# Exchanging the two hardware DMA queues of a softmax mixture: loads from ScalarE, stores from SyncE

## Chip, cores, metric

One core of a Trainium2 chip. The metric is device time in microseconds (us), lower is better. The time of the kernel before was 780.9 us (median of 3, 780.88 to 781.12).

## The reference

```python
# logits (32, 128, 4, 4096) f32, prior (32, 128, 4) f32 -> out (32, 128, 4096) f32
prior_probs = softmax(prior, axis=-1)
mixture = np.sum(prior_probs[..., None] * softmax(logits, axis=-1), axis=2)
```

Each of 4096 rows has four heads of 4096 logits. 268.4 MB come in, 67.1 MB go out.

## The kernel before

The rows are cut into 32 tiles (`U`) of 128 rows. A tile is loaded as 128 rows of 64 KB, four exponentials on ScalarE give the heads and their sums, VectorE weighs and adds them into an output tile, and a store sends that out. Logits and output tiles have two buffers each. SyncE and ScalarE each have a queue (also called a ring) of transfers of their own; a transfer lands when its completion is signalled, and a packet in the profile's counts is here one contiguous row, or piece of a row, of a transfer (plus 16 tiny ones each). Waits are put in by hand: `only(ins, *keep)` lets an instruction wait for `keep` and nothing else.

```python
    def load(u):
        if u == 0 or u >= U - 3:                     # first and last tiles come in pieces
            cuts = (0, 2, 3, 4) if u == U - 1 else (0, 2, 4)
        else:
            cuts = (0, H)
        for h, to in zip(cuts, cuts[1:]):
            ld = nc.sync.dma_start(out=ltile[:, u % 2, h:to], in_=lg[u // J, u % J, :, h:to, :])
            if u >= 2:
                only(ld, adds[u - 2, 0] if h == 0 else exps[u - 2, to - 1])
            ...
    def store(u, acc, eng, lo=0, hi=V):
        st = eng.dma_start(out=ov[u // J, u % J, :, lo:hi], in_=acc[:, lo:hi])
        stores[u] = only(st, adds[u, H - 1])
    ...
        for u in range(U):
            ...
            free = (stores[u - 2],) if bufd and u >= 2 else ()
            m = H if u < U - 4 else 2                # the last four tiles work in pairs of heads
            for h in range(H):
                late = h == H - 1 and 4 <= u < U - 3
                if h == H - 1 and 0 < u < U - 3:
                    store(u - 1, obuf[:, (u - 1) % 2], nc.scalar)
                exp(h, *((stores[u - 4],) if late else ()))
                ...
                mul = weigh(g, m, *(free if g == 0 else ()))   # GpSimd; waits for the output tile
                ...                                            # then the adds, on VectorE
            if u + 2 < U:
                load(u + 2)
            if u == U - 3:                           # tiles 28, 29: stores on SyncE,
                store(u - 1, obuf[:, (u - 1) % 2], nc.sync)    # behind the last loads
                store(u, acc, nc.sync)
            elif u == U - 2:
                store(u, acc, nc.sync)
```

The softmax here doesn't subtract the row's maximum and nothing guards it: scores larger than these inputs give would overflow.

## Time and profile before

| | before |
|---|---|
| median time; span of the profiled run | 780.9; 779.3 us |
| bytes, mean rate over the span | 335.66 MB, 431 GB/s |

The prediction below shows the lines of the profile, and reads from them what bounds the kernel.

### The profile page before, as it was taken

What the parts mean: (1) busy time and instruction counts of PE and PEld (TensorE: products, weight loads), DVE (VectorE), ACT (ScalarE), POOL (GpSimd) and SP (SyncE); (2) the same over time, 40 slices, a digit from 0 to 9 for tenths busy, and PEclk for the clock granted to TensorE, in tenths of its full rate; (3) what the DMA queues carried; (4) which work ended last, traced back from release to release, by engine and by line L of the source; (5) the groups of instructions that cost most, each with busy time, mean ns of one, the idle gap of its engine ahead of it and who ended that gap; (6) DMA issues with size and microseconds to landing.
All of it is one profiled execution on the core that took longest, in us unless ns stands there. A gap on an engine that the chain in (4) does not pass through costs nothing.

```text
span 779.3 us, 654 instructions
## 1 busy us (share of the span) xinstructions
DVE 521.0 (67%) x174; ACT 466.7 (60%) x258; POOL 8.3 (1%) x41
## 2 busy tenths in 40 slices
DVE  4447875558755587555775557855578655689886
ACT  4476555775457755577555675546765567657782
POOL 0000000000000000000000000000000000000000
DMA  9999999999999999999999999999999999999998
GB/s 407 457 417 401 470 407 434 428 461 428 405 467 403 458 420 433 442 443 418 431 454 407 454 408 467 420 415 447 432 442 417 463 399 463 410 427 433 434 429 377
DMA packets 10117, 335.66 MB, mean 431 GB/s; under 512 B 1136, under 2 KB 1136, under 8 KB 1152
## 3 DMA queue, kind: packets, MB, share of 16 engines
q1 hardware_dynamic: 6048, 276.83, 82.3%
q10 hardware_dynamic: 4064, 58.79, 17.6%
q14 instruction: 5, 0.04, 0.0%
HBM read 268.50 MB, written 67.11 MB: 431 GB/s over the span
## 4 chain that ended last, share of the span: by engine, by line
DMA 64%; ACT 27%; DVE 6%; issue 2%; POOL 0%; DVEq 0%; POOLq 0%
DMA ltile<-in_logits_dram 62%; ACT ebuf L159 19%; ACT ltile L159 8%; DVE obuf L177 5%; DMA out_dram<-obuf 2%; DVE ltile L183 1%; POOL coeff L170 0%; DVE rden L168 0%; DVEq L240 0%; POOLq L240 0%; POOLq L170 0%
## 5 line engine op out<-in xcount | busy, mean ns | idle before, releaser
L183 DVE SCALAR_TENSOR_TENSOR obuf<-ebuf,coeff,obuf 128x4096 f32<-128x4096 f32 x90 | 403.6, 4484 | 3.8 <-POOL coeff L170 0.6
L159 ACT ACTIVATE ebuf<-ltile 128x4096 f32<-128x4096 f32 x90 | 322.9, 3589 | 7.4 <-DMA ltile<-in_logits_dram 7.4
L159 ACT ACTIVATE ltile<-ltile 128x4096 f32<-128x4096 f32 x38 | 137.3, 3614 | 280.6 <-DMA ltile<-in_logits_dram 280.6
L168 DVE RECIPROCAL rden<-dsum 128x4 f32<-128x4 f32 (+1 forms) x36 | 6.3, 175 | 227.9 <-ACT ebuf L159 225.1
L177 DVE TENSOR_SCALAR obuf<-ltile,coeff 128x4096 f32<-128x4096 f32 x30 | 70.6, 2353 | 10.2 <-POOL coeff L170 10.2
L183 DVE SCALAR_TENSOR_TENSOR ltile<-ltile,coeff 128x4096 f32<-128x4096 f32 (+1 forms) x7 | 27.0, 3875 | 0.8 <-POOL coeff L170 0.6
L159 ACT ACTIVATION_READ_ACCUMULATOR ebuf<-ltile 128x1 f32 x90 | 16.8, 186 | 0.0
L170 POOL TENSOR_TENSOR coeff<-rden,pp 128x4 f32<-128x4 f32 (+1 forms) x36 | 7.2, 200 | 755.3 <-DVE rden L168 745.4
L159 ACT ACTIVATION_READ_ACCUMULATOR ltile<-ltile 128x1 f32 x38 | 7.1, 186 | 0.0
L139 DVE TENSOR_REDUCE pmax<-pr 16x256 f32<-16x1024 f32 x1 | 1.2, 1208 | 7.8 <-DMA pr<-in_prior_dram 7.8
L141 ACT ACTIVATE pr<-pr 16x1024 f32<-16x1024 f32 x1 | 1.1, 1055 | 7.8 <-DVE pr L140 7.8
L177 DVE TENSOR_SCALAR ltile<-ltile,coeff 128x4096 f32<-128x4096 f32 x2 | 4.7, 2354 | 0.6 <-POOL coeff L170 0.6
L144 DVE TENSOR_TENSOR pn<-pr,pmax 16x1024 f32<-16x1024 f32 x1 | 1.9, 1939 | 0.1
L141 ACT ACT_TABLE_LOAD x1 | 1.3, 1283 | 1.2 <-PEq L229 1.2
L142 DVE TENSOR_REDUCE pmax<-pr 16x256 f32<-16x1024 f32 x1 | 1.2, 1207 | 1.1 <-ACT pr L141 1.1
L149 DVE STREAM_TRANSPOSE pp<-pn 32x256 f32<-32x256 f32 x4 | 1.7, 435 | 0.1
L143 DVE RECIPROCAL pmax<-pmax 16x256 f32<-16x256 f32 x1 | 1.7, 1741 | 0.0
L140 DVE TENSOR_TENSOR pr<-pr,pmax 16x1024 f32<-16x1024 f32 x1 | 1.2, 1211 | 0.0
L138 POOL MEMSET pn<- 32x1024 f32 x1 | 0.9, 941 | 0.3 <-POOLq L229 0.3
L229 POOL MEMSET const-bfloat16-1.0<- 128x1 bf16 x1 | 0.1, 106 | 0.0
L229 POOL MEMSET const-uint8-127<- 128x1 uint8 x1 | 0.1, 106 | 0.0
L229 POOL MEMSET const-float32-0.0<- 128x1 f32 x1 | 0.1, 103 | 0.2 <-issue 0.2
(1 smaller groups left out, 0.1 us busy)
## 6 DMA issues: line engine op xcount, KB each, us to landing
out_dram<-obuf ACTq DMA_DIRECT2D x28, 2048.0 KB, 29.4
ltile<-in_logits_dram SPq DMA_DIRECT2D x7, 4096.0 KB, 26.1
ltile<-in_logits_dram SPq DMA_DIRECT2D x2, 2048.0 KB, 30.9
out_dram<-obuf SPq DMA_DIRECT2D x2, 2048.0 KB, 33.9
out_dram<-ltile SPq DMA_DIRECT2D x1, 2048.0 KB, 17.2
out_dram<-ltile SPq DMA_DIRECT2D x2, 1024.0 KB, 4.8
ltile<-in_logits_dram SPq DMA_DIRECT2D x28, 30.9
pr<-in_prior_dram ACTq DMA_DIRECT2D x1, 64.0 KB, 7.0
```

Source lines behind the costliest of these rows:

```text
L139: nc.vector.reduce_max(pmax, pr, axis=AX.X)
L140: nc.vector.tensor_sub(pr, pr, pmax.unsqueeze(2).to_broadcast([G, R, H]))
L141: nc.scalar.activation(pr, pr, AF.Exp)
L142: nc.vector.reduce_sum(pmax, pr, axis=AX.X)
L143: nc.vector.reciprocal(pmax, pmax)
L144: nc.vector.tensor_mul(pn[0:G].rearrange("g h r -> g r h"), pr, pmax.unsqueeze(2).to_broadcast([G, R, H]))
L149: nc.vector.transpose(pp[32 * t : 32 * (t + 1)], pq[:, :, :, 32 * t : 32 * (t + 1)])
L159: ex = nc.scalar.activation(es[h], lt[:, h], AF.Exp, accum_out=dsum[:, u, h : h + 1])
L168: rc = nc.vector.reciprocal(rden[:, u, h : h + n], dsum[:, u, h : h + n])
L170: mul = nc.gpsimd.tensor_mul(coeff[:, u, h : h + n], rden[:, u, h : h + n], ppu[:, h : h + n])
L177: st = nc.vector.tensor_scalar(out=acc[:, lo:hi], in0=es[h][:, lo:hi], scalar1=coeff[:, u, h : h + 1], scalar2=None, op0=ALU.mult,)
L183: st = nc.vector.scalar_tensor_tensor(out=acc[:, lo:hi], in0=es[h][:, lo:hi], scalar=coeff[:, u, h : h + 1], in1=acc[:, lo:hi], op0=ALU.mu ...
```

## The change

The intent is to let ScalarE issue the loads and SyncE the stores and the prior, to send the first transfer of both queues ahead of the start barrier, and to wait for the output tile in the fourth exponential and not in GpSimd's coefficient.

```diff
-            ld = nc.sync.dma_start(
+            ld = nc.scalar.dma_start(
...
-        nc.scalar.dma_start(out=pr, in_=pv)
+        nc.sync.dma_start(out=pr, in_=pv)
...
-                late = h == H - 1 and 4 <= u < U - 3
-                if h == H - 1 and 0 < u < U - 3:
-                    store(u - 1, obuf[:, (u - 1) % 2], nc.scalar)
-                exp(h, *((stores[u - 4],) if late else ()))
+                if h == 2 and 0 < u < U - 3:
+                    store(u - 1, obuf[:, (u - 1) % 2], nc.sync)
+                exp(h, *(free if m == H and h == H - 1 else ()))
...
-                mul = weigh(g, m, *(free if g == 0 else ()))
+                mul = weigh(g, m, *(free if m < H and g == 0 else ()))
```

The line of the store now stands before the third exponential and not the fourth, in SyncE's program; the fourth exponential's wait for the store of four tiles ago is gone. The rest of the diff (cut) moves the first transfer of ScalarE, as well as that of SyncE, ahead of the barrier. The three lines that issue the stores of tiles 28 to 30 are not touched: they say SyncE before and after.

More of the change, by code (lines that the diff above doesn't have):

```diff
@@ L11, with early_transfers, of @@
 AX = mybir.AxisListType
-def early_first_load(nc):
+def early_transfers(nc):
     blocks = nc.main_func.blocks
-    first = next(
-        (b, i)
-        for b in blocks[1:]
-        for i in b.instructions
-        if i.engine == mybir.EngineType.SP and i.opcode == "DMACopy"
-    )
-    block, ins = first
-    assert not ins.sync_info.on_wait
-    block.instructions.remove(ins)
-    at = next(
-        n
-        for n, i in enumerate(blocks[0].instructions)
-        if i.engine == mybir.EngineType.SP and i.opcode == "Drain"
-    )
-    blocks[0].instructions.insert(at, ins)
+    def of(block, engine, opcode):
+        return next(
+            (i for i in block.instructions if i.engine == engine and i.opcode == opcode), None
+        )
+    for engine in (mybir.EngineType.SP, mybir.EngineType.Activation):
+        body = next(b for b in blocks[1:] if of(b, engine, "DMACopy"))
+        ins = of(body, engine, "DMACopy")
+        assert not ins.sync_info.on_wait
+        body.instructions.remove(ins)
+        drain = of(blocks[0], engine, "Drain")
+        blocks[0].instructions.insert(blocks[0].instructions.index(drain), ins)
 @with_exitstack
@@ L46 @@
     nc = tc.nc
-    nc.at_finalize(early_first_load)
+    nc.at_finalize(early_transfers)
     B, S, H, V = logits.shape
```

## The prediction

> **What bounds the kernel now.** I read the page's busy shares and DMA rows first, then the chain of waits, then one steady tile (a tile is 128 rows; there are 32) in the stretch table, the timeline and the queue table, and last the end of the run.
>
> ```profile
> DVE 521.0 (67%) x174; ACT 466.7 (60%) x258; POOL 8.3 (1%) x41
> ...
> DMA  9999999999999999999999999999999999999998
> ...
> DMA packets 10117, 335.66 MB, mean 431 GB/s; under 512 B 1136, under 2 KB 1136, under 8 KB 1152
> ...
> DMA 64%; ACT 27%; DVE 6%; issue 2%; POOL 0%; DVEq 0%; POOLq 0%
> ```
>
> No compute engine is above 67%; the DMA engines are full in 39 of 40 slices. One tile moves 8.39 MB in and 2.10 MB out. The stretch table of two steady tiles (columns: stretch, length, DVE, ACT, POOL busy, clock, DMA share, GB/s) and the queue rows of the first of them:
>
> ```profile
> 400.00:424.18 24.18, 15.99 (x6) 14.51 (x8) 0.20 (x1) 1.00 1.00 434
> 424.18:448.36 24.18, 15.99 (x6) 14.50 (x8) 0.20 (x1) 1.00 1.00 434
> ```
> ```profile
> q1 hardware_dynamic: 144, 8.39, 80.0%
> q10 hardware_dynamic: 144, 2.10, 20.3%
> ```
>
> The period is 24.18 us: 10.49 MB at 434 GB/s. q1 is SyncE's queue (loads), q10 ScalarE's (stores). Both send 144 packets, yet 8.39 against 2.10 MB: the queues take turns packet by packet. A full load has one packet per row of 64 KB, a store one of 16 KB (128 of each and 16 tiny ones a tile), so a store gets one fifth, and a 2.10 MB store needs the whole tile period. The timeline of one tile:
>
> ```profile
> 403.21 3.62 ACT L159 ACTIVATE ltile<-ltile 128x4096 f32<-128x4096 f32 x1 [9.67 <-DMA ltile<-in_logits_dram]
> ...
> 410.01 0.34 ACTq L113 DMA_DIRECT2D out_dram<-obuf  x1
> ...
> 414.02 3.60 ACT L159 ACTIVATE ebuf<-ltile 128x4096 f32<-128x4096 f32 x1
> ...
> 418.00 0.20 POOL L170 TENSOR_TENSOR coeff<-rden,pp 128x4 f32<-128x4 f32 x1 [23.97 <-DVE rden L168]
> 418.24 2.35 DVE L177 TENSOR_SCALAR obuf<-ltile,coeff 128x4096 f32<-128x4096 f32 x1 [0.32 <-POOL coeff L170]
> 420.62 24.50 SPq L100 DMA_DIRECT2D ltile<-in_logits_dram  x2
> ```
>
> The load lands at 403.2, four exponentials follow, the next load is issued at 420.62 after the first DVE operation. The load already in flight lands at 427.39 (the next tile's first ACTIVATE), so a load is issued 6.8 us before the queue of loads would be empty: that is the slack. The store goes out at 410.01, when the previous tile's last add ends; it lands 29.4 us later.
>
> **What the Trainium skill says.** "DMA: Bandwidth & Descriptors", section "Queues, rings and completion order": SyncE and ScalarE each own a ring on the same 16 engines, and an engine takes turns between rings a packet at a time. The trace agrees (144 and 144 packets above). Same page, "Issuing engines are not separate DMA queues": starting transfers from several engines saves only issue time; an issue here is 0.34 us on ScalarE and 0.33 on SyncE. Same page, "Where 436 GB/s comes from": a ceiling of 435.2 GB/s; the trace has 434, so no more than 0.3% is left in the steady part. "Advanced Engine Details and Errata", section "Engine Queue Depths": ScalarE has 8 entries; the trace agrees that its sequencer runs ahead of its datapath (the store at 410.01 was issued before the exponential ahead of it in the program began, at 410.43).
>
> **The change part by part.**
>
> *Queues in the steady part.* Bytes, packet sizes and turns are the same with the names exchanged: 0 us. A store on SyncE waits for the same last add: 0 us. A load on ScalarE stands after the tile's fourth exponential and waits for the same DVE operation, which needs that exponential anyway; it holds the sequencer until 420.62, but the next exponential cannot start before 427.39: 0 us.
>
> *The wait for the output buffer* (store of two tiles ago) moves from GpSimd's coefficient (418.00) to the fourth exponential (414.02). That store was issued a period before the one at 410.01, at 385.83, and lands at 385.83 + 29.4 = 415.2. GpSimd passed it with 2.8 us to spare; the exponential will wait 1.2 us, in some 26 tiles, some 30 us in total. The next load's slack falls from 6.8 to 5.6 us: nothing on the path. It does not build up: landings of stores are paced by DMA, and an issue 1.2 us later only shortens its wait behind the previous store (29.4 becomes 28.2). The floor is the 27.4 us of the first store, which met an empty store queue; from the fourth exponential to the next store is 434.19 - 414.02 = 20.2, and 27.4 + 20.2 = 47.6, under two periods, 48.4. Close, but closed: 0 to 2 us.
>
> *Both early transfers.* The prior lands at 7.8 now and is used long before tile 0 is weighed at 30; the first load is issued at 0.00 either way: 0 us.
>
> *The end* is where I expect a cost. Before, the stores of tiles 28 to 31 are issued from SyncE, behind the last loads in the same ring. Now they have a ring of their own and take turns with those loads, which moreover come in halves (32 KB packets, turns 2:1) and quarters (16 KB, 1:1). Before, by its timeline and the landing times:
>
> ```profile
> 720.12 3.59 ACT L159 ACTIVATE ebuf<-ltile 128x4096 f32<-128x4096 f32 x1 [5.00 <-DMA ltile<-in_logits_dram]
> ...
> 727.84 9.48 SPq L113 DMA_DIRECT2D out_dram<-obuf  x2
> ...
> 729.78 3.62 ACT L159 ACTIVATE ltile<-ltile 128x4096 f32<-128x4096 f32 x1 [2.35 <-DMA ltile<-in_logits_dram]
> ...
> 739.50 3.62 ACT L159 ACTIVATE ltile<-ltile 128x4096 f32<-128x4096 f32 x1 [2.41 <-DMA ltile<-in_logits_dram]
> ...
> 749.22 3.62 ACT L159 ACTIVATE ltile<-ltile 128x4096 f32<-128x4096 f32 x1 [2.41 <-DMA ltile<-in_logits_dram]
> ...
> 760.03 3.60 ACT L159 ACTIVATE ltile<-ltile 128x4096 f32<-128x4096 f32 x1
> ...
> 764.29 9.13 DVE L183 SCALAR_TENSOR_TENSOR ltile<-ltile,coeff 128x4096 f32<-128x4096 f32 x3 [0.31 <-POOL coeff L170]
> ```
>
> Load halves land 9.7 us apart (4.19 MB alone at 434), the last quarter at about 749.2 + 2 x 4.83 = 758.9; the four stores then drain while the last heads are computed. Now I rework it with 9.66 us for a half, 4.83 for a quarter or a store, 2 us from a store's issue to its first bytes, turns as above (all estimates from these rows):
> - Store 28 is ready when tile 28's last add ends, 717.5 before, 718.2 now; it runs beside the first half of load 30 from 720.1. At 2:1 both need 14.5 us: that half lands at 734.6 (before 729.8).
> - Store 29 is ready at 737.0 as before, runs from 739. Second half of load 30: 4.5 us alone, the other 5.16 at 2:1 in 7.7, lands at 746.8 (before 739.5). First half of load 31: 6.8 us beside the rest of store 29, then 5.2 alone: 758.7 (before 749.2).
> - Tile 30's last two exponentials run 746.8 to 754.1, its last two adds end at 0.5 + 9.0 later, 763.6; store 30 runs from 765.6.
> - Third quarter of load 31 at 763.5. Last: 2.15 us alone, the other 2.68 at 1:1 with store 30 in 5.4: 771.0 (before 758.9, so 12 us later: stores 28 and 29, 9.7 us, and 2.7 us of store 30).
> - Then nothing is left to hide behind: exponential 3.7, reciprocal and coefficient 0.5, adds 9.1 end at 784.4, last store 4.8, close 1.0: 790.2 against 779.3.
>
> DMA has about 9 us without data, from the end of store 30 (773.1) to the first half of store 31 at 782.1. Sum: +10.9 us in the end, +0 to 2 in the steady part, so about 791.5 for a measured 780.9.
>
> **The rivals.** (a) Nothing moves: bytes are the same and DMA is full, 780 to 782. For it: 434 GB/s everywhere. Against it: the end is only full because stores are kept back. (b) The new wait feeds back: if the floor of 27.4 us were more by 0.8, each pair of tiles would lose what is over; with the whole 1.2 us lost per pair, 13 pairs give 16 us on top of the end, about 807. Against it: an empty store queue gives all bandwidth to the loads, so nothing need be lost. (c) Loads issued by a busy ScalarE come late and DMA runs dry: it would need over 6.8 us of delay a tile; I see 1.2. (d) The end costs less, since a store that starts sooner frees DMA later: about 785 if half of it is regained; the last exponential cannot start before its load, though. Faster by 2% would need 765.3, under 335.66 MB at 435.2 GB/s (771.3).
>
> **Range and chances.** Centre 791.5. Low 783: the end mostly absorbed. High 797: the end a little worse (more of store 30 ahead of the last quarter) with 2 to 3 us from the new wait. Slower by over 2% begins at 796.5: 0.12. Faster: 0.01. Within 2%: 0.87.
>
> **What would show it.** Right: steady period still 24.2 us at 434 GB/s; a ScalarE wait for a store, about 1.2 us in some 26 tiles, and stores landing in 28.2; POOL's waits for stores only in the end; loads of tile 30 landing at about 735 and 747, of tile 31 at 759 to 771; a DMA hole of some 9 us in the last 20. Wrong: a longer steady period or dips of DMA between tiles (b or c), or a last slice as full as before with the last load at 759 (a).

## The result

The changed kernel takes 790.87 us (median of 4, 790.84 to 791.06) against 781.01 for the kernel before in the same rounds: a ratio of 1.0126, 95% interval 1.011 to 1.0141. All outputs are right.

The page of the changed kernel, DMA row and rates in 40 slices:

```profile
span 789.1 us, 676 instructions
...
DMA  9999999999999999999999999999999999999993
GB/s 402 452 412 452 412 452 412 452 407 457 412 462 401 453 424 453 407 457 442 409 462 416 430 420 462 404 470 405 458 402 455 412 462 405 449 424 425 435 428 162
```

In the DMA row only the last slice differs: it is at 3 tenths, 162 GB/s, where the kernel before had 8 tenths and 377. The waits (engine, operation, releaser; total, times, longest) show the moved wait, and it is small:

```profile
ACT ebuf L157 <- DMA out_dram<-obuf: 30.7, 25, 1.5
...
POOL coeff L168 <- DMA out_dram<-obuf: 10.7, 1, 10.7
```

The page's chain of work that ended last now runs through the landings of stores (46% of the span, 2% before), which makes this wait look like the cause. The second experiment below shows that it is not.

The stretch table (stretch, length, DVE, ACT, POOL busy, clock, DMA share, GB/s), two steady tiles and then the end:

```profile
400.00:424.18 24.18, 15.99 (x6) 14.62 (x8) 0.20 (x1) 1.00 1.00 434
424.18:448.36 24.18, 15.78 (x6) 14.62 (x8) 0.20 (x1) 1.00 1.00 434
...
757.00:771.00 14.00, 10.39 (x5) 11.22 (x7) 0.20 (x1) 1.00 1.00 428
771.00:774.00 3.00, 2.76 (x1) 3.00 (x1) 0.00 (x0) 1.00 0.26 109
774.00:783.00 9.00, 8.22 (x4) 0.40 (x2) 0.20 (x1) 1.00 0.05 21
```

The steady part is as it was. Between 774 and 783 the DMA engines do almost nothing (share 0.05). In the kernel before they were still at 0.99 from 770 to 775 and ran dry near 777:

```profile
770.00:775.00 5.00, 3.42 (x2) 0.00 (x0) 0.00 (x0) 1.00 0.99 415
```

The timeline tells why the hole comes; the lines are the starts of the exponentials that waited for the pieces of the last two loads, and the last adds:

```profile
734.24 3.62 ACT L157 ACTIVATE ltile<-ltile 128x4096 f32<-128x4096 f32 x1 [6.59 <-DMA ltile<-in_logits_dram]
...
746.36 3.62 ACT L157 ACTIVATE ltile<-ltile 128x4096 f32<-128x4096 f32 x1 [4.82 <-DMA ltile<-in_logits_dram]
...
759.07 3.62 ACT L157 ACTIVATE ltile<-ltile 128x4096 f32<-128x4096 f32 x1 [5.40 <-DMA ltile<-in_logits_dram]
...
770.69 3.62 ACT L157 ACTIVATE ltile<-ltile 128x4096 f32<-128x4096 f32 x1 [0.71 <-DMA ltile<-in_logits_dram]
...
774.91 9.14 DVE L181 SCALAR_TENSOR_TENSOR ltile<-ltile,coeff 128x4096 f32<-128x4096 f32 x3 [0.31 <-POOL coeff L168]
```

The pieces that the kernel before had at 729.8, 739.5 and 749.2 arrive at 734.2, 746.4 and 759.1, and its last exponential, which began at 760.0, begins at 770.7 and had to wait for its load. By then the stores that could have filled the queues have been sent.

Where the 9.8 us of span went: up to the first exponential -0.5 us (12.15 against 12.66); from the exponentials of tile 1 to those of tile 28, 652.45 us against 651.69, +0.8; from there to the end, 95.4 against 85.9, +9.6 (rounded). The border between the last two is not sharp: in the second experiment, which takes the wait away and has the same span, the three terms are -0.4, 0.0 and +10.2 us.

### The profile page after: what moved, and what is told of

Read it like the earlier page. It is cut to its first block, busy times and chain, and to the rows that moved or that the text cites. A ratio compares the mean times of both kernels' runs of the same rounds, so it can differ in the third digit from the quotient of the medians.

```text
span 789.1 us, 676 instructions
## 1 busy us (share of the span) xinstructions
DVE 521.0 (66%) x174; ACT 469.7 (60%) x258; POOL 8.4 (1%) x41
## 4 chain that ended last, share of the span: by engine, by line
DMA 60%; DVE 28%; ACT 9%; issue 2%; POOL 0%; DVEq 0%; ACTq 0%; POOLq 0%
DMA out_dram<-obuf 46%; DVE obuf L181 22%; DMA ltile<-in_logits_dram 14%; ACT ebuf L157 8%; DVE obuf L175 4%; ACT ltile L157 1%; DVE ltile L181 1%; POOL coeff L168 0%; DVE rden L166 0%; DVEq L239 0%; ACTq L98 0%; POOLq L239 0%; ACTq L157 0%
## 5 line engine op out<-in xcount | busy, mean ns | idle before, releaser
L157 ACT ACTIVATE ebuf<-ltile 128x4096 f32<-128x4096 f32 x90 | 323.4, 3593 | 37.6 <-DMA out_dram<-obuf 30.7
L157 ACT ACTIVATION_READ_ACCUMULATOR ebuf<-ltile 128x1 f32 x90 | 16.8, 186 | 0.0
## 6 DMA issues: line engine op xcount, KB each, us to landing
out_dram<-obuf SPq DMA_DIRECT2D x30, 2048.0 KB, 28.1
```

The lines of the kernel that those rows point to most:

```text
L157: ex = nc.scalar.activation(es[h], lt[:, h], AF.Exp, accum_out=dsum[:, u, h : h + 1])
```

## The experiments

The theory: the whole cost is that the stores of tiles 28 to 30 take turns with the last loads. The rivals: the wait on ScalarE, or the exchange of the queues itself. "Changed" is the changed kernel, "before" the kernel before.

### The late stores held back

```diff
 # changed; keep=() is passed on to only(...) in store
-                store(u - 1, obuf[:, (u - 1) % 2], nc.sync)
+                store(u - 1, obuf[:, (u - 1) % 2], nc.sync, keep=(loads[U - 1, 2],))
                 store(u, acc, nc.sync)
```

> The changed kernel, with one wait added: the store of tile 28 (and so those of 29 and 30, which follow it on SyncE) is not issued before the third quarter of the last load has landed, about 754 us. Theory (the whole cost is that the late stores take turns with the last loads): loads of tiles 30 and 31 land as in the kernel before, 729.8, 739.5, 749.2 and the last at 759 to 760, the hole of about 9 us in DMA closes, and the time returns to 780.5 to 782. Rival (the cost comes from the swapped queues or from the new wait on ScalarE in the steady part): stays at 789 to 791.

Measured: 781.45 us (781.35 to 781.65) against 781.0, ratio 1.0006 (0.9991 to 1.0021). Its timeline:

```profile
729.99 3.62 ACT L157 ACTIVATE ltile<-ltile 128x4096 f32<-128x4096 f32 x1 [2.34 <-DMA ltile<-in_logits_dram]
...
739.70 3.62 ACT L157 ACTIVATE ltile<-ltile 128x4096 f32<-128x4096 f32 x1 [2.40 <-DMA ltile<-in_logits_dram]
...
749.41 3.62 ACT L157 ACTIVATE ltile<-ltile 128x4096 f32<-128x4096 f32 x1 [2.40 <-DMA ltile<-in_logits_dram]
...
754.34 0.81 SPq L111 DMA_DIRECT2D out_dram<-obuf  x2
```

The loads land where they did before (730.0, 739.7, 749.4), the stores leave together at 754.3, the last exponential begins at 760.4 (760.0 before), and the stretch from 765 to 770 has a DMA share of 0.99 again. Queues stay exchanged and the wait stays on ScalarE; taking the stores out of the loads' way gives the time back. A wait added made the kernel 9.4 us faster.

### The wait back on GpSimd

```diff
 # changed
-                exp(h, *(free if m == H and h == H - 1 else ()))
+                exp(h, *((stores[u - 4],) if h == H - 1 and 4 <= u < U - 3 else ()))
...
-                mul = weigh(g, m, *(free if m < H and g == 0 else ()))
+                mul = weigh(g, m, *(free if g == 0 else ()))
```

> The changed kernel with the wait for the output tile put back on GpSimd's coefficient, as in the kernel before (and the fourth exponential waiting for the store of four tiles ago). Theory: ScalarE's 25 waits of 1.2 us for stores vanish and stores land in about 29.4 us again, but the time stays at 790 to 791.5, since those waits are not on the path. Rival (the waits, 30.7 us in all, are the 9.9 us): falls to 781 to 785.

Measured: 791.05 us (791.01 to 791.13). ScalarE has no wait for a store any more, stores land in 29.4 us again, and the time is that of the changed kernel. Tile 1 to tile 28 takes 651.7 us (41.35 to 693.05), so the 0.8 us of the steady part do come from the wait; yet tile 29's third exponential starts at 720.42, and at 720.34 in the changed kernel. My reading, which no run tests by itself: the loads had been ahead only because the stores were further behind, and the full DMA engines evened that out. The 0.8 us do not show in the time.

### Before, with the late stores in a ring of their own

```diff
 # before; the store of tile 28 stays where it is, but from ScalarE
+                if u == U - 2 and h == 2:
+                    store(u - 1, obuf[:, (u - 1) % 2], nc.scalar)
+                if u == U - 1 and h == 3:
+                    store(u - 1, ltile[:, (u - 1) % 2, 0], nc.scalar)
                 exp(h, *((stores[u - 4],) if late else ()))
...
-                store(u - 1, obuf[:, (u - 1) % 2], nc.sync)
-                store(u, acc, nc.sync)
-            elif u == U - 2:
-                store(u, acc, nc.sync)
+                store(u - 1, obuf[:, (u - 1) % 2], nc.scalar)
```

> The kernel before with one thing changed: the stores of tiles 28, 29 and 30 go out from ScalarE, so that they have a ring of their own beside the last loads on SyncE. They stand in ScalarE's program where it is not held up by them. Theory: the last load lands at about 770 instead of 759, a DMA hole of some 9 us opens and the time is 789 to 791. Rival (the swap of loads and stores matters): stays within 2 us of 781.

Measured: 790.35 us (790.25 to 790.37), ratio 1.0119 (1.0104 to 1.0134). The kernel before, nothing exchanged, no wait moved, shows the same loss when three stores change their ring. The pieces of the last loads land at 732.7, 746.0, 758.7, the last exponential begins at 769.7, and the hole is there:

```profile
771.00:774.00 3.00, 2.63 (x3) 2.42 (x2) 0.20 (x1) 1.00 0.27 115
774.00:783.00 9.00, 8.96 (x3) 0.00 (x0) 0.00 (x0) 1.00 0.16 67
```

### Smaller packets in the late stores: a first try that missed

```diff
 # changed; likewise for the stores of tiles 29 and 30
-                store(u - 1, obuf[:, (u - 1) % 2], nc.sync)
+                for c in range(4):
+                    store(u - 1, obuf[:, (u - 1) % 2], nc.sync, c * V // 4, (c + 1) * V // 4)
```

> The changed kernel with the stores of tiles 28 to 30 cut into four column quarters each, so that their rows are 4 KB instead of 16 KB. Theory (queues take turns packet by packet): beside 32 KB load packets a store then gets one ninth instead of a third, beside 16 KB ones one fifth instead of a half, and the last load lands at about 765 instead of 771; the time is 784 to 786. Rival (queues share by bytes, or a store's bytes come first however they are cut): the last load stays at 771 and the time at 790 to 792.

Measured: 792.51 us (792.49 to 792.58), slower than the changed kernel. The expectation fails, but not at the turns. From 722 to 734 us the queue rows (queue, packets, MB, share of 16 engines), this kernel first, then the changed one:

```profile
q10 hardware_dynamic: 159, 4.69, 90.4%
q1 hardware_dynamic: 159, 0.59, 11.9%
```
```profile
q10 hardware_dynamic: 113, 3.18, 61.4%
q1 hardware_dynamic: 126, 2.06, 40.1%
```

The packets are again one for one, and the loads get nine tenths where the changed kernel gave them six. What spoiled the run is another wait:

```profile
743.61 0.82 ACTq L98 DMA_DIRECT2D ltile<-in_logits_dram  x2
744.48 3.62 ACT L157 ACTIVATE ltile<-ltile 128x4096 f32<-128x4096 f32 x1 [16.82 <-DMA out_dram<-obuf]
```

The build hands eight completion semaphores to all transfers in turn. With nine transfers more, the last two quarters of the load have to wait, in the built program, for two earlier transfers that hold their semaphores: a piece of the store of tile 28, and the second half of the load of tile 30. They were issued only at 743.6 (in the changed kernel at 724.1 and 727.7), and ScalarE, whose program has these loads ahead of its next exponential, stood for 16.8 us, put down by the profile to a store's landing.

### Smaller packets with fewer transfers

```diff
 # changed; two transfers per late store, each of two 4 KB blocks per row
+    def store4(u, acc):
+        cut = lambda ap: ap.rearrange("p (a c w) -> p c a w", a=2, c=2)
+        for c in range(2):
+            st = nc.sync.dma_start(out=cut(ov[u // J, u % J])[:, c], in_=cut(acc)[:, c])
+            stores[u] = only(st, adds[u, H - 1])
...                                    # used for tiles 28, 29, 30
```

> The test of the packet turns again, without the semaphores that held up the last two loads in the run with quarters: the stores of tiles 28 to 30 go out as two transfers each, each of two blocks of 4 KB per row, so rows of 4 KB as before but half the transfers. Theory (turns packet by packet): a store gets one ninth beside 32 KB load packets and one fifth beside 16 KB ones, the last load lands at about 765 instead of 771, and the time is 784 to 786. Rival (bytes are shared, however cut): last load at 771, time 790 to 792.

Measured: 785.59 us (785.55 to 785.87), ratio 1.0059 (1.0044 to 1.0075). From 722 to 730 us:

```profile
q10 hardware_dynamic: 109, 3.11, 90.1%
q1 hardware_dynamic: 110, 0.45, 13.7%
```

109 packets against 110. One shared semaphore is left: the last quarter is issued at 731.3 and not at 727.7, after the first half of the load of tile 30 has landed, but the next exponential (731.7) needed that half too. The pieces land at 731.7, 742.3, 753.3 and the last exponential begins at 765.6. The same bytes on the same queues, with rows of 4 KB and not 16 KB, give back 5.3 us: the share of a queue follows its packet size.

### One store beside the loads, two held

```diff
 # changed; store takes keep=() as above
                 store(u - 1, obuf[:, (u - 1) % 2], nc.sync)
-                store(u, acc, nc.sync)
+                store(u, acc, nc.sync, keep=(loads[U - 1, 2],))
```

> The changed kernel with only the stores of tiles 29 and 30 held until the third quarter of the last load has landed; the store of tile 28 still runs beside the loads. Theory (each store that goes ahead of the last load moves it by its own 4.83 us): load halves of tile 30 at about 734.5 and 744, last load at about 764, and the time 784 to 786, about half way between the held version (781.5) and the changed kernel (790.9). Rival (all or nothing): 781 or 790.

Measured: 785.63 us (785.56 to 785.74), ratio 1.006. The pieces land at 734.3, 744.6, 754.3, and the last exponential begins at 765.3. The cost comes in parts: 4.2 us for the store of tile 28 (785.63 less the 781.45 of all held), 5.2 for those of tiles 29 and 30 together (790.87 less 785.63).

### The wait one exponential earlier

```diff
 # changed
-                exp(h, *(free if m == H and h == H - 1 else ()))
+                exp(h, *(free if m == H and h == H - 2 else ()))
```

> The changed kernel with the wait for the output tile one exponential earlier (the third instead of the fourth), so that ScalarE would wait 1.2 + 3.6 = 4.8 us a tile at first. Rival b of the prediction in full (the wait feeds back on itself): 27.4 us for a store and 23.8 from the third exponential to the next store are 51.2, so two tiles take 51.2 instead of 48.4, some 36 us in all, about 825. Theory (a store that runs while no load is queued gets all bandwidth, so landings come sooner and DMA stays full): 790 to 794, stores landing in about 24.5 us.

Measured: 826.37 us (822.65 to 827.37), ratio 1.0573 (1.0552 to 1.0594). My theory is wrong here and the rival's number is right. The waits, and two starts of the exponential that waits:

```profile
ACT ebuf L157 <- DMA out_dram<-obuf: 115.2, 14, 10.8
ACT ltile L157 <- DVE obuf L175: 36.8, 11, 3.4
```
```profile
409.80 3.59 ACT L157 ACTIVATE ebuf<-ltile 128x4096 f32<-128x4096 f32 x1 [8.43 <-DMA out_dram<-obuf]
...
420.07 0.33 ACTq L98 DMA_DIRECT2D ltile<-in_logits_dram  x1
...
459.97 3.59 ACT L157 ACTIVATE ebuf<-ltile 128x4096 f32<-128x4096 f32 x1 [8.42 <-DMA out_dram<-obuf]
```

The store of the tile whose exponential waited until 409.80, alone, with its landing:

```profile
433.57 20.51 SPq L111 DMA_DIRECT2D out_dram<-obuf  x2
```
```profile
DMA to landing us min/median/max: 26.3/26.3/26.3
```

The wait comes 14 times, from 100 us on in every other tile. It goes round the loop of rival b: 23.8 us from the exponential that waited to the issue of that tile's store (409.80 to 433.57), and 26.3 us until this store lands and frees the next such exponential (459.97). These two tiles take 50.2 us; the twelve pairs from 100.32 to 716.63 take 51.4 us on average, where the rival had 51.2 and the kernel before 48.4. Half of my argument holds: a store that runs while little or no load is queued is quick (from 415 to 420 the store queue has 95 of the 112 packets). But these are the stores of the tiles between, which land in 18.0 to 19.8 us from 97.6 us on and for which nothing waits; those that are waited for take 26.0 to 30.0, and the median of all, 19.7, hides this. Both queues run empty meanwhile: the next load is issued at 420.07, ten microseconds after the wait ends, and between 422 and 424 the DMA share is 0.08. From 200 to 700 us each stretch of 100 us runs at 404 to 408 GB/s. So the loop feeds back as the rival added it up, with some 3 us lost per pair of tiles. The changed kernel stands one exponential, 3.6 us, from this.

### Before, with the early prior

The edit moves the first transfer of ScalarE (the prior) ahead of the barrier, with the function of the changed kernel.

```diff
 # before
-    nc.at_finalize(early_first_load)
+    nc.at_finalize(early_transfers)
```

> The kernel before with only the early transfer of the prior added. In the changed kernel the first exponential started at 12.15 instead of 12.66. If that comes from the prior going first, this run has it too and takes 780.4 to 780.8; if it comes from the loads being on ScalarE's queue, it stays at 781.0.

Measured: 780.85 us (780.81 to 781.03) against 780.93, ratio 0.9999 (0.9987 to 1.0012). The first exponential starts at 12.70, as in before. The load still goes first in this run (at 0.00, the prior at 0.13), where the changed kernel sends the prior at 0.00 and the load at 0.12. So the 0.5 us at the start do not come from this alone; whether from the order or from the ring, I did not try to tell. No version here beats the kernel before, and with 335.66 MB at 434 GB/s taking 773.4 us (an estimate from the steady rate), only some 6 us of its span of 779.3 lie outside full transfer, which bounds what a further change of order could gain.

## Why the prediction was right

The main step was right, and the time close (790.9 for 791.5). That it is so close is in part luck, for the terms do not add up to 791.5: 780.9 + 10.9, with 0 to 2 more, gives 791.8 to 793.8. The measured time is 0.9 to 2.9 us under this sum.

- *Queues in the steady part, 0 us*: confirmed; the tile still takes 24.18 us at 434 GB/s, and the first experiment keeps the exchange and loses nothing.
- *The moved wait, 1.2 us in some 26 tiles, 0 to 2 us in all*: 25 waits, 30.7 us, stores landing in 28.1. It costs nothing: with it taken away the time was 791.05.
- *It does not build up*: right for this kernel, with the reason only half right. Rival b was dismissed because "an empty store queue gives all bandwidth to the loads, so nothing need be lost". The run with the wait one exponential earlier shows that something is lost: 35 us. The other half of the step, 47.6 against two periods of 48.4, is what fits both kernels: the same sum with 23.8 for 20.2 gives 51.2 where 51.4 was measured. The changed kernel is on the safe side by a margin of only 0.8 us, on which I should have leaned alone.
- *The end, +10.9 us*: measured +9.6, or +10.2 in the run without the wait. The pieces came within 0.5 us of the reworked times (734.2, 746.4, 759.1, 770.7 for 734.6, 746.8, 758.7, 771.0). The predicted span was 790.2, the measured one 789.1. Most of this 1.1 us is in the last term: the final store was given the 4.8 us of before, and took 4.0, now that the queues before it were empty (share 0.05). The 2 us from a store's issue to its first bytes come out of none of the lines shown; the first half of the last store was issued at 781.8 and the first bytes move at 782.6, so 0.8 us. That the pieces came so close all the same means that something offset it; what, I did not trace.
- *Both early transfers, 0 us*: the start came 0.5 us sooner, which the prediction did not have; the prior landed at 2.3 instead of 7.8, which helped nobody.
- *Rival a* falls with the hole, *rival c* with the steady rate, *rival d* with the measured end.

## What to carry over

When a kernel is bound by transfers, look at which transfers a piece of work that is still to come depends on, and let those go first: at the end that means loads ahead of stores, and stores kept as filling for the time in which only compute is left. In these runs one queue keeps that order for free (in the kernel before, the stores issued at 727.8 and 737.0, behind the last loads, landed some 34 us later, and the pieces of the loads came 9.7 us apart all the while); two queues took turns packet by packet, so the one with longer rows got more. After a change of queues, recheck the transfers that the diff does not touch.

## What the Trainium skill lacked or had wrong

- "DMA: Bandwidth & Descriptors", "Issuing engines are not separate DMA queues", says that issuing on several engines saves only issue time. In these runs the choice of the engine also sets the order: three stores moved from behind the loads to the other ring cost 9.4 us of 781 (790.35 against 781.0). The page has the two halves of this under "Queues, rings and completion order" (a ring is consumed in order, rings take turns), but does not draw the conclusion.
- Same page, "Queues, rings and completion order": turns by packets agree with the trace, but a packet is given there as some 9 to 17 descriptors, and nothing is said of the share that follows. Here the turns went by rows of 64, 32, 16 and 4 KB, one for one (144 to 144, 159 to 159, 109 to 110), so bytes split by row length (8.39 to 2.10 MB for 64 to 16 KB, 4.69 to 0.59 MB for 32 to 4 KB).
- No page gives the cost in time of completion semaphores that a build shares between the transfers of both queues: here nine more transfers held up two loads, and with them ScalarE, for 16.8 us.
